# Banded attention heads in a fused transformer layer: where the division, the sinks, the low key halves and a norm are computed

## The chip, the cores and the metric

The kernel runs on one core of a Trainium2 chip. The core has five engines that run side by side and wait for each other by semaphores: TensorE (PE, matrix products into PSUM), VectorE (DVE), ScalarE (ACT), GpSimd (POOL) and SyncE (SP, which here only issues transfers). The metric is the device time of one launch in microseconds (us), lower is better.

## The reference, cut to what matters

One layer: modulated norm, one input projection, two groups of attention heads, output projection, residual, second modulated norm, and a mixture of 32 experts of which each token uses four. There are 512 tokens and 256 context tokens, width 1024. The change concerns the second group of heads, eight query heads over two key heads, banded, with a sink logit per head:

```python
s_loc = einsum('bnqkgd,bnjkd->bnkgqj', qbk, kband)      # own block of 128 tokens and its neighbours
s_ctx = einsum('bnqkgd,bjkd->bnkgqj', qbk, k_ctx)       # all 256 context tokens
s_loc = where(valid, s_loc, MASK_VALUE)
p = softmax(concatenate([s_loc, s_ctx, sink_col], -1), -1)   # the sink only enters the sum
o = einsum(p_loc, vband) + einsum(p_ctx, v_ctx)
...
x = x + g1 * (concatenate([ya, yb], -1) @ w_out)
hx2 = modulate(rmsnorm(x, norm2_g), sh2, sc2)           # then router logits, top 4 of 32
```

## The kernel before, in words

All products are in fp32 accuracy from parts: a value is split into a high part (a rounding copy, ScalarE) and a low part (the difference, VectorE), and the products of the parts are added in PSUM. Weights go through the same split.

The launch has three stretches. First the modulation, the input projection and the four global heads. Then the stage of the banded heads, in which the output projection, the second norm and the router of the blocks already finished run along. Last the experts: for each, 24 weight tiles of 1024 columns are split by ScalarE and VectorE and multiplied by TensorE, while the SP queue loads the next ones into buffers as they come free.

The banded stage walks through sixteen units (n, m): n is a block of 128 tokens, m a pair of the eight query heads. A unit of block 0 or 3 has 512 keys, one of block 1 or 2 has 640. `scores_B` makes a unit's scores: for each of two heads and each cut of the keys (256 and 256, or 256, 256 and 128 for the first head and 256 and 384 for the second with 640 keys) a product with the high keys on 128 rows (`kB[:, g]`, to which the queries hold both their halves) and one with the low keys on the 64 rows on which they lie (`kB[rw, 2]`), then masks in bf16. A one-column copy of the sink goes beside the scores, then maximum, exponential with its sum, reciprocal, and the scaling of the probabilities, on VectorE for one head and on ScalarE for the other. The tiles `sc` (scores) and `o` (values) exist once in PSUM, `tp` (transposes) and `pj` (projections) twice. `turn_B` transposes the probabilities two key blocks at a time and splits them, `mix_B` multiplies them with the values, `put_B` adds the two halves of a finished pair of units into `yB` and splits the result for the output projection. `start_Y` splits the global heads' rows for the same product.

A loop over the units makes the next unit's scores while it turns and mixes the current one, and puts the output projection's parts (`out_proj`, one of eight row blocks kb), and the steps `norm2`, `route_T`, `route` and `rank` of the block before, in between. The scheduler reorders each engine's instructions by a model of the machine, with the written order as priority; only what is marked with `keep_in_program_order` or pinned stays put. The two last row blocks of block 3's projection, and all that prepares the first expert, stand behind the loop and are pinned. The new helper names in the diff replace these functions.

Of the kernel before, what the change touches and what calls it, by code (L numbers as in the profile page):

```python
# [10 lines left out]
F32 = mybir.dt.float32  # L11
F32R = mybir.dt.float32r
# [10 lines left out]
T = 512  # L23
# [14 lines left out]
def tile_block(ctx: ExitStack, tc: tile.TileContext, a: dict, out: bass.AP, dbg=None):  # L38
# [64 lines left out]
    def ps_pj():  # L103
        return ps.tile([128, 512], F32, name="pj", bufs=2)
# [704 lines left out]
    def scores_B(n, m):  # L809

        b0, b1 = max(n - 1, 0), min(n + 2, 4)
        L = (b1 - b0) * 128
        nk = C + L
        g = m // 2
        rw = slice(g * 64, g * 64 + 64)
        q = qT[n]
        own = n + m < KN["own"]
        if own:
            assert nk == 512
            sv = [ps_pj() for _ in range(2)]  # L820
        else:
            s = sc_tile(KN["sB"])
            sv = [s[:, 0:TA], s[:, TA:2 * TA]]
        for i in range(2):
            hd, s = 2 * m + i, sv[i]
            cuts = [(0, C), (C, nk)] if i == 1 or nk == 512 else [(0, C), (C, 512), (512, nk)]
            masks = []
            if n > 0:
                masks.append((mprev, C))
            if n < 3:  # L830
                masks.append((mnext, nk - 128))
            ksl = lambda x0, x1: slice(T + x0, T + x1) if x0 < C else slice(b0 * 128 + x0 - C, b0 * 128 + x1 - C)
# [8 lines left out]
        nm = bp.tile([128, 2], F32, name="nmB", bufs=4)  # L841
        rs = bp.tile([128, 2], F32, name="rsB", bufs=4)
        w = nk if own else nk + 1
        for i in range(0 if own or KN["snk"] == "P" else 2):
            (V.tensor_copy if KN["snk"][i] == "V" else S.copy)(sv[i][:, nk:w], sinkB[:, 2 * m + i:2 * m + i + 1])
        for i in range(2):
            V.tensor_reduce(nm[:, i:i + 1], sv[i][:, 0:w], axis=AX.X, op=OP.max, negate=True)
        if own:
            es = bp.tile([128, 3, 2], F32, name="esB", bufs=1)
            V.tensor_scalar_mul(es[:, 0], sinkB[:, 2 * m:2 * m + 2], -1.0)  # L850
            V.tensor_tensor(nm, nm, es[:, 0], op=OP.min)
            V.tensor_add(es[:, 1], nm, sinkB[:, 2 * m:2 * m + 2])
            S.activation(es[:, 2], es[:, 1], AF.Exp)
        pp = []
        for i in range(2):
            p = bp.tile([128, 641], F32, name="pB", bufs=5)
            S.activation(p[:, 0:w], sv[i][:, 0:w], AF.Exp, bias=nm[:, i:i + 1], accum_out=rs[:, i:i + 1])
            pp.append(p)
        if own:
            V.tensor_add(rs, rs, es[:, 2])  # L860
        V.reciprocal(rs, rs)
        for i in range(2):
            if KN["scB"][i] == "S":
                S.activation(pp[i][:, 0:nk], pp[i][:, 0:nk], AF.Copy, scale=rs[:, i:i + 1])
            else:
                (V if KN["scB"][i] == "V" else G).tensor_scalar(pp[i][:, 0:nk], pp[i][:, 0:nk], rs[:, i:i + 1], 1.0,
                                                             op0=OP.mult, op1=OP.mult)
        return pp, [4, 5] + list(range(b0, b1))

    def turn_B(pp, bl):  # L870

        w = len(bl) * 256
        tp = ps_tp().rearrange("p a b -> p (a b)")
        for i, x in enumerate(bl):
            for j in range(2):
                PE.transpose(tp[:, (2 * i + j) * 128:(2 * i + j + 1) * 128], pp[j][:, x * 128:(x + 1) * 128], ident)
        pt = pair(bp, [128, 512], "pT", 2)
        split(pt[0][:, 0:w], pt[1][:, 0:w], tp[:, 0:w])
        return pt
# [49 lines left out]
    cur = scores_B(0, 0)  # L929
# [72 lines left out]
    Gt = lp.tile([128, E], F32, name="Gt")  # L1002
# [10 lines left out]
    fill = lp.tile([128, E * 3], F32, name="fill")  # L1013
    V.memset(fill, 0.0)
# [19 lines left out]
    zt = lp.tile([128, D], F32, name="t1", bufs=2)  # L1034
    V.memset(zt, 0.0)
    dma(acc[T:T + 128, :], zt)
# [20 lines left out]
    def norm2(t):  # L1057
        t1 = lp.tile([128, D], F32, name="t1", bufs=2)
        for f in range(2):
            add_out(t, f, t1)  # L1060
        late = V if t == 3 else G
        gp2(t1, x1[t], G2B, OP.mult)
        sq = lp.tile([128, 4, 128], F32, name="ya", bufs=1).bitcast(BF16).rearrange("p a b -> p (a b)")
        ss = lp.tile([128, 1], F32, name="ss2", bufs=2)
        rs = lp.tile([128, 1], F32, name="rs2", bufs=2)
        S.activation(sq, x1[t], AF.Square, accum_out=ss)
        rstd_of(rs, ss, D)

        rt[t] = t1, rs, late
# [53 lines left out]
    def enter_slots(t):  # L1123
        eq, mi, ge, gs, pr = rt.pop(t)
        pk = lp.tile([128, 4, E], F32, name="pk")
# [13 lines left out]
        V.tensor_mul(eq, eq, val[:, :, 1:2].to_broadcast([128, 4, E]))  # L1139
        V.tensor_reduce(Gt, eq.rearrange("p k e -> p e k"), axis=AX.X, op=OP.add)  # L1140
# [29 lines left out]

    for i, (n, m) in enumerate(units):
        nxt = scores_B(*units[i + 1]) if i < 15 else None
        if m % 2 == 0:
            o = ps_o()
        pp, blocks = cur
        if m == 0 and n > 0:
            start_Y(n)
        if n == 0 and m == KN["ys"][0]:
            start_Y(n, slice(0, KN["yh"]))
        if n == 0 and m == KN["ys"][1]:  # L1180
            start_Y(n, slice(KN["yh"], 4))
# [12 lines left out]
        if m % 2 == 1:  # L1194
            put_B(m // 2, o, Yt[n][1])
# [3 lines left out]
        if n == 0 and m == 2:  # L1199
            router_vectors()  # L1200
# [4 lines left out]
        if n > 0:  # L1205
            (norm2, route_T, route, rank)[m](n - 1)
# [4 lines left out]
        if m == 3 and n < 2:  # L1211
            load_qB(n + 2)
    most = mo.tile([1, 1], I32, name="most")
# [644 lines left out]
```

## Time and profile before

| | us |
|---|---|
| median of three timed runs | 1682.74 |
| lowest and highest of them | 1678.67, 1683.17 |
| the profiled execution | 1678.89 |
| its span, first to last instruction | 1677.1 |
| banded stage in it | 285 to 457 |

Times inside the profile count from the first instruction. An engine's busy time is the sum of its instructions' durations, which for TensorE overlap, so the start of the next one is the better measure there. PEld is TensorE's loading of the stationary operand. Most instructions carry line 52, a helper through which they are all recorded, and are told apart by the tiles that they write and read (out<-in).

### The profile page before, as it was taken

How to read it: one execution, taken by the hardware profiler on the slowest of the kernel's cores; microseconds unless marked ns; L12 is line 12 of the kernel's file. 1: busy time of each engine (PE TensorE's matmuls, PEld its weight loads, DVE VectorE, ACT ScalarE, POOL GpSimd, SP SyncE). 2: the span in 40 equal slices, each digit the busy share in tenths (PEclk: the TensorE clock that was granted, in tenths of full speed). 3: DMA queues.
4: the chain of work that ended last, by engine and by line, in shares of the span. 5: the costliest groups of instructions: out<-in, count | busy, mean ns of one | idle time of the engine just before them, and what ended most of it. 6: DMA issues, size and time to landing. Idle time of an engine off the chain costs nothing. (4 is left out here: it accounts for less than half of the span.)

```text
span 1677.1 us, 20947 instructions
## 1 busy us (share of the span) xinstructions
PE 1601.9 (96%) x7464; PEld 1283.1 (77%) x7464; DVE 1482.5 (88%) x1753; ACT 1093.5 (65%) x1406; POOL 213.6 (13%) x136
## 2 busy tenths in 40 slices
PE   7899997899889999999999999999999999999995
PEld 2686775677677888888888888888888888888884
DVE  6888887556778999999999999999999999999995
ACT  6544434445556767777776777776777777677763
POOL 0000001012330111111111111111111111111011
PEclk9899997879979999999999999999999999999998
DMA  9534325611579999999999999999999999999974
GB/s 350 173 92 132 108 88 149 184 45 47 193 244 380 353 367 369 357 377 372 374 362 366 360 369 380 383 362 366 369 362 369 374 374 361 367 355 370 357 295 128
DMA packets 115698, 494.11 MB, mean 295 GB/s; under 512 B 16385, under 2 KB 39082, under 8 KB 68418
## 3 DMA queue, kind: packets, MB, share of 16 engines
q1 hardware_dynamic: 99090, 456.44, 71.2%
q0 software_dynamic: 14192, 29.00, 8.4%
q10 hardware_dynamic: 2304, 7.24, 1.2%
q8 instruction: 61, 1.00, 0.2%
q14 instruction: 51, 0.42, 0.1%
HBM read 472.91 MB, written 27.57 MB: 298 GB/s over the span
## 5 line engine op out<-in xcount | busy, mean ns | idle before, releaser
L52 PE MATMUL h<-two 128*128 128x512 f32 x1694 | 421.5, 400 | 3.0 <-ACT two L52 3.0
L52 PEld LDWEIGHTS h<-two 128*128 128x128 f32 x1694 | 315.3, 189 | 74.3 <-ACT two L52 3.9
L52 PE MATMUL h<-wp,two 128*128 128x512 f32 x1338 | 334.7, 400 | 4.1 <-DVE pk L52 4.1
L52 DVE TENSOR_TENSOR two<-wp,two 128x1024 fp32r<-128x1024 f32 x254 | 300.8, 1219 | 7.5 <-ACT two L52 7.4
L52 PEld LDWEIGHTS h<-wp,two 128*128 128x128 f32 x1338 | 249.1, 190 | 58.2 <-ACT two L52 4.3
L52 ACT CAST two<-wp 128x1024 fp32r<-128x1024 f32 x254 | 258.0, 1049 | 17.0 <-PE y L52 14.6
L52 DVE TENSOR_TENSOR wp<-wp 128x1024 fp32r<-128x1024 f32 x176 | 205.5, 1219 | 2.9 <-ACT wp L52 2.9
L52 DVE TENSOR_TENSOR two<-w,two 128x1024 fp32r<-128x1024 f32 x170 | 200.2, 1219 | 2.3 <-ACT two L52 2.3
L52 POOL DMA_INDIRECT acc<-ys,slot_i x31 | 105.5, 3403 | 704.6 <-DVE ys L52 704.6
L52 ACT CAST wp<-wp 128x1024 fp32r<-128x1024 f32 x176 | 176.2, 1050 | 12.2 <-PE y L52 7.1
L52 ACT CAST two<-w 128x1024 fp32r<-128x1024 f32 x170 | 170.2, 1049 | 13.3 <-PE y L52 10.5
L52 PE MATMUL y<-two,ah 128*128 128x512 f32 x556 | 174.6, 395 | 0.8 <-DVE w L52 0.8
L52 PE MATMUL y<-wp,ah 128*128 128x512 f32 x468 | 147.1, 395 | 0.4 <-DVE wp L52 0.4
L52 DVE TENSOR_TENSOR wp<-w,wp 128x1024 fp32r<-128x1024 f32 x104 | 125.5, 1218 | 8.4 <-ACT wp L52 8.3
L52 PEld LDWEIGHTS y<-two,ah 128*128 128x128 f32 x556 | 104.4, 188 | 26.1 <-DVE w L52 1.2
L52 ACT CAST wp<-w 128x1024 fp32r<-128x1024 f32 x104 | 108.7, 1049 | 23.4 <-PE pj L52 10.3
L52 ACT CAST ah<-tpm 128x512 fp32r<-128x512 f32 x64 | 37.6, 588 | 123.1 <-PE tpm L52 123.1
L52 PE MATMUL y<-two,al 128*128 128x512 f32 x278 | 109.9, 395 | 0.0
L52 PEld LDWEIGHTS y<-wp,ah 128*128 128x128 f32 x468 | 88.2, 188 | 21.3 <-DVE wp L52 0.6
L52 DVE TENSOR_TENSOR wp<-wchunk,wp 128x1024 fp32r<-128x1024 f32 x82 | 98.2, 1218 | 0.0
L52 PE MATMUL pj<-xh,wp 128*128 128x512 f32 (+1 forms) x320 | 91.7, 364 | 1.9 <-ACT xf L52 1.0
L52 PE MATMUL y<-wp,al 128*128 128x512 f32 x234 | 92.4, 395 | 0.0
(333 smaller groups left out, 2350.1 us busy)
## 6 DMA issues: line engine op xcount, KB each, us to landing
wp<-in_w_gate_up_dram SPq DMA_DIRECT2D x140, 1024.0 KB
w<-in_w_gate_up_dram SPq DMA_DIRECT2D x85, 1024.0 KB
wp<-in_w_down_dram SPq DMA_DIRECT2D x75, 1024.0 KB
w<-in_w_down_dram SPq DMA_DIRECT2D x43, 1024.0 KB
wchunk<-in_w_gate_up_dram SPq DMA_DIRECT2D x31, 1024.0 KB
wm<-in_w_mod_dram SPq DMA_DIRECT2D x64, 256.0 KB
wchunk<-in_w_down_dram SPq DMA_DIRECT2D x10, 1024.0 KB
w<-in_w_in_dram SPq DMA_DIRECT2D x14, 512.0 KB
```

Source lines behind the costliest of these rows:

```text
L52: i = f(*args, **kwargs)
```

## The change

- The low keys get a tile of their own, `klB`, padded with zeros to 128 rows for each key head, and the second score product reads all 128 rows.
- The sink column is written by a small matmul (three bf16 parts of the sink on rows 0, 32 and 64, against ones), in all units but the first.
- The probabilities are not scaled any more. `put_B` takes the reciprocals of four heads' sums, broadcasts them by four transposes into a `tp` tile, and multiplies the finished values.
- The second norm's factor (`norm2_factor`) is computed one unit later than its square sum.
- Small tiles of the router share buffers, a zero tile is smaller and is read twice.
- `Scores` and `Turned` replace `scores_B` and `turn_B` by steps that the loop calls one by one; the loop puts them, and the steps of projection, norm and router, in another order.

```diff
+    klB = bp.tile([128, 2, TA], F32R, name="klB")
+    for g in range(2):
+        rw, ro = slice(g * 64, g * 64 + 64), slice(64 - g * 64, 128 - g * 64)
+        G.memset(klB[ro, g].bitcast(F32), 0.0)
+        S.copy(klB[rw, g], kB[rw, 2].bitcast(F32))
...
             for x0, x1 in cuts:
                 PE.matmul(s[:, x0:x1], q[:, hd], kB[:, g, ksl(x0, x1)], start=True, stop=False)
-                PE.matmul(s[:, x0:x1], q[rw, hd], kB[rw, 2, ksl(x0, x1)], start=False, stop=not mk)
+                PE.matmul(s[:, x0:x1], q[:, hd], klB[:, g, ksl(x0, x1)], start=False, stop=not mk)
-            if not own and KN["snk"] == "P":
+            if not self.own:
                 PE.matmul(s[:, nk:nk + 1], ones3, sink3[:, hd:hd + 1], start=True, stop=True)
-        for i in range(0 if own or KN["snk"] == "P" else 2):
-            (V.tensor_copy if KN["snk"][i] == "V" else S.copy)(sv[i][:, nk:w], sinkB[:, 2 * m + i:2 * m + i + 1])
...
-        V.reciprocal(rs, rs)
-        for i in range(2):
-            if KN["scB"][i] == "S":
-                S.activation(pp[i][:, 0:nk], pp[i][:, 0:nk], AF.Copy, scale=rs[:, i:i + 1])
-            else:
-                (V if KN["scB"][i] == "V" else G).tensor_scalar(pp[i][:, 0:nk], pp[i][:, 0:nk], rs[:, i:i + 1], 1.0,
-                                                             op0=OP.mult, op1=OP.mult)
...
+        def exp(self, i):
+
+            p = bp.tile([128, 641], F32, name="pB", bufs=4)
+            S.activation(p[:, 0:self.w], self.sv[i][:, 0:self.w], AF.Exp, bias=self.nm[:, i:i + 1], accum_out=self.rs[:, i:i + 1])
+            self.pp.append(p)
...
+    class Turned:
+
+
+        def __init__(self, pp, bl):
+            self.w = len(bl) * 256
+            self.tp = ps_tp().rearrange("p a b -> p (a b)")[:, 0:self.w]
+            for i, x in enumerate(bl):
+                for j in range(2):
+                    PE.transpose(self.tp[:, (2 * i + j) * 128:(2 * i + j + 1) * 128], pp[j][:, x * 128:(x + 1) * 128], ident)
+
+        def high(self):
+            self.pt = pair(bp, [128, 512], "pT", 2)
+            S.copy(self.pt[0][:, 0:self.w], self.tp)
+
+        def low(self):
+            V.tensor_tensor(self.pt[1][:, 0:self.w], self.tp, self.pt[0][:, 0:self.w].bitcast(F32), op=OP.subtract)
...
-    def put_B(g, o, y):
+    def put_B(n, g, o, y):
...
+        rs = sums[n, g]
+        V.reciprocal(rs, rs)
+        rb = ps_tp()
+        for j in range(4):
+            PE.transpose(rb[:, j, :], rs[:, j:j + 1].to_broadcast([128, 128]), ident)
         S.copy(yb[0:64], ov[64:128, 0::2, :])
         S.copy(yb[64:128], ov[0:64, 1::2, :])
         V.tensor_add(yb[0:64], ov[0:64, 0::2, :], yb[0:64])
         V.tensor_add(yb[64:128], ov[64:128, 1::2, :], yb[64:128])
+        V.tensor_mul(yb[0:64], yb[0:64], rb[0:64, 0::2])
+        V.tensor_mul(yb[64:128], yb[64:128], rb[64:128, 1::2])
         fb = slice(4 + 2 * g, 6 + 2 * g)
         split(y[:, 0, fb], y[:, 1, fb], yb)
...
-    cur = scores_B(0, 0)
+    cur = Scores(0, 0)
...
-    fill = lp.tile([128, E * 3], F32, name="fill")
-    V.memset(fill, 0.0)
+    zt = lp.tile([128, 4, 128], F32, name="hT", bufs=1).rearrange("p a b -> p (a b)")
+    V.memset(zt, 0.0)
+    fill = zt[:, 0:E * 3]
...
-    zt = lp.tile([128, D], F32, name="t1", bufs=2)
-    V.memset(zt, 0.0)
-    dma(acc[T:T + 128, :], zt)
+    dma(acc[T:T + 128, :].rearrange("p (a f) -> p a f", a=2), zt[:, None, :].to_broadcast([128, 2, 512]))
...
+        S.activation(sq, x1[t], AF.Square, accum_out=ss)
+        rt[t] = t1, ss, late
+
+    def norm2_factor(t):
+        t1, ss, late = rt[t]
         rs = lp.tile([128, 1], F32, name="rs2", bufs=2)
-        S.activation(sq, x1[t], AF.Square, accum_out=ss)
         rstd_of(rs, ss, D)
...
-        lg = lp.tile([128, E], F32, name="lg", bufs=2)
+        lg = lp.tile([128, E], F32, name="lg", bufs=1)
...
-        pk = lp.tile([128, 4, E], F32, name="pk")
+        pk = lp.tile([128, 4, 128], F32, name="hT", bufs=1)[:, 0].rearrange("p (k e) -> p k e", k=4)
...
+        Gt = lp.tile([128, E], F32, name="lg", bufs=1)
...
-        nxt = scores_B(*units[i + 1]) if i < 15 else None
+        nxt = Scores(*units[i + 1]) if i < 15 else None
...
-        pp, blocks = cur
-        if m == 0 and n > 0:
-            start_Y(n)
-        if n == 0 and m == KN["ys"][0]:
-            start_Y(n, slice(0, KN["yh"]))
-        if n == 0 and m == KN["ys"][1]:
-            start_Y(n, slice(KN["yh"], 4))
+        pp, blocks = cur.pp, cur.blocks
         fill = [(n - 1, 6), (n - 1, 7)] if m == 0 else [(n, 2 * m - 2), (n, 2 * m - 1)]
-        if n == 0:
-            fill = [(0, kb) for kb in KN["f0"][m]]
+        if n + m == 0:
+            fill = []
         bls = [list(range(x, min(x + 2, len(blocks)))) for x in range(0, len(blocks), 2)]
-        pts = [turn_B(pp, bl) for bl in bls[:2]]
-        for k, bl in enumerate(bls):
-            if k == 2:
-                pts.append(turn_B(pp, bl))
-            if k < len(fill):
-                out_proj(fill[k][0], [fill[k][1]])
-            mix_B(m, pts[k], bl, blocks, o)
-        cur = nxt
-        if m % 2 == 1:
-            put_B(m // 2, o, Yt[n][1])
+        if nxt:
+            for k in range(2):
+                nxt.head(k)
+            for k in range(2):
+                nxt.max(k)
+        ts = [Turned(pp, bl) for bl in bls[:2]]
+        for k in range(2):
+            ts[k].high()
+            if nxt:
+                nxt.exp(k)
+        for k in range(2):
+            ts[k].low()
+        if m != 1:
+            for f in fill[0:1]:
+                out_proj(f[0], [f[1]])
+        mix_B(m, ts[0].pt, bls[0], blocks, o)
+        if len(bls) > 2:
+            ts.append(Turned(pp, bls[2]))
+            ts[2].high()
+            ts[2].low()
+
+        if m == 0:
+            start_Y(n, slice(0, 4 if n else 3))
+        if (n, m) == (0, 2):
+            start_Y(n, slice(3, 4))
         if n == 0 and m < 3:
             prep_out(2 * m + 2)
             prep_out(2 * m + 3)
-        if n == 0 and m == 2:
+        if (n, m) == (0, 3):
             router_vectors()
         if n > 1 and m == 0:
             turn_gates(n - 2)
             start_acc(n - 2, ps_tp)
             load_x1(n)
-        if n > 0:
-            (norm2, route_T, route, rank)[m](n - 1)
+        if n > 0 and m == 1:
+            norm2(n - 1)
+        if n > 0 and m == 2:
+            norm2_factor(n - 1)
+            route_T(n - 1)
+        if n > 0 and m == 3:
+            route(n - 1)
+        if m != 1:
+            for f in fill[1:2]:
+                out_proj(f[0], [f[1]])
+        for k in range(1, len(bls)):
+            mix_B(m, ts[k].pt, bls[k], blocks, o)
+        if m == 1:
+            for f in fill:
+                out_proj(f[0], [f[1]])
+        if m % 2 == 1:
+            put_B(n, m // 2, o, Yt[n][1])
+        if n > 0 and m == 3:
+            rank(n - 1)
+        cur = nxt
         if m == 2 and n < 3:
             load_Y(n + 1)
             if n == 0:
                 load_x1(1)
         if m == 3 and n < 2:
             load_qB(n + 2)
+    pinned[0] = ""
```

## Rows read from the trace of the kernel before

**Rows 1.** The page, busy time of each engine over the whole span (share of the span, instructions).

```profile
PE 1601.9 (96%) x7464; PEld 1283.1 (77%) x7464; DVE 1482.5 (88%) x1753; ACT 1093.5 (65%) x1406; POOL 213.6 (13%) x136
```

**Rows 2.** Busy time of each engine in stretches (from:to, length, busy us and instructions of each engine, granted TensorE clock as a share of 2.4 GHz, DMA share, GB/s): the banded stage, three slices of it, a slice of the experts.

```profile
285.00:457.00 172.00, 157.35 (x803) 121.93 (x802) 111.34 (x259) 87.92 (x200) 31.75 (x30) 0.90 0.37 115
285.00:295.00 10.00, 7.87 (x38) 5.64 (x37) 8.65 (x16) 4.90 (x10) 0.00 (x0) 0.84 0.45 145
335.00:345.00 10.00, 8.69 (x32) 5.99 (x31) 6.15 (x10) 5.88 (x12) 0.00 (x0) 0.58 0.19 60
415.00:425.00 10.00, 8.92 (x63) 7.21 (x61) 6.35 (x23) 5.10 (x15) 0.00 (x0) 1.00 0.09 26
1000.00:1010.00 10.00, 10.00 (x48) 8.27 (x47) 9.38 (x10) 7.54 (x10) 1.33 (x1) 1.00 1.02 390
```

**Rows 3.** Who waited for whom (us in total, times, longest): TensorE in the banded stage, its two longest entries, and the SP queue from 500 to 1640 us.

```profile
PE sc L52 <- ACT pB L52: 2.3, 5, 0.8
PE o L52 <- DVE pTl L52: 2.3, 5, 0.7
...
SPq L1257 <- DVE two L52: 316.5, 127, 5.3
```

**Rows 4.** Matmuls in order of time, at full clock (start, us from the first start to the last end of the merged ones, instruction, count). First a chain of value products (the first and the last of five that follow each other), then groups of score products and masks of two units.

```profile
365.52 0.27 PE L52 MATMUL o<-pTl,vB 128*128 128x256 f32 x1
...
365.99 0.28 PE L52 MATMUL o<-pTl,vB 128*128 128x256 f32 x1
...
319.02 1.32 PE L52 MATMUL sc<-kB,qB 128*128 128x256 f32 x4 [0.47 <-ACT pB L52]
320.27 0.23 PE L52 MATMUL sc<-mprev,identb 128*128 128x128 bf16 x1
320.31 0.56 PE L52 MATMUL sc<-kB,qB 128*128 128x128 f32 x2
320.80 0.23 PE L52 MATMUL sc<-mnext,identb 128*128 128x128 bf16 x1
...
368.76 1.42 PE L52 MATMUL sc<-kB,qB 128*128 128x256 f32 x4
370.10 0.23 PE L52 MATMUL sc<-mprev,identb 128*128 128x128 bf16 x1
```

**Rows 5.** Groups of instructions in the banded stage (count, busy us, mean ns of one, idle time before them and its causes).

```profile
L52 PE MATMUL sc<-kB,qB 128*128 128x256 f32 (+5 forms) x136 | 47.8, 406 | 2.3 <-ACT pB L52 2.3
L52 PE MATMUL o<-pTh,vB 128*128 128x256 f32 x72 | 23.4, 338 | 2.6 <-DVE yB L52 1.3 <-ACT pTh L52 1.1
L52 ACT ACTIVATE pB<-pB,rsB 128x512 f32<-128x512 f32 (+1 forms) x16 | 12.5, 780 | 4.6 <-DVE rsB L52 4.6
L52 DVE TENSOR_SCALAR pB<-pB,rsB 128x512 f32<-128x512 f32 (+1 forms) x16 | 9.5, 597 | 0.3
L52 DVE TENSOR_TENSOR yB<-o,yB 64x256 f32<-64x256 f32 x16 | 6.7, 422 | 7.9 <-ACT yB L52 7.5
L52 DVE COPY sc<-sinkB 128x1 f32<-128x1 f32 x15 | 2.4, 163 | 15.4 <-PE sc L52 15.3
L52 PE MATMUL tp<-bdr,GtT 96*128 96x512 f32 x4 | 1.4, 398 | 0.0
```

**Rows 6.** Score products in order of time in the half-clock stretch.

```profile
338.87 2.30 PE L52 MATMUL sc<-kB,qB 128*128 128x256 f32 x4
341.11 0.29 PE L52 MATMUL sc<-mprev,identb 128*128 128x128 bf16 x1
```

**Rows 7.** Score products of a global head in order of time: two on 128 rows, two on 64, and the next.

```profile
262.54 0.61 PE L52 MATMUL sc<-kh,q 128*128 128x512 f32 x2 [2.11 <-ACT p L52]
263.08 0.61 PE L52 MATMUL sc<-kl,q 64*128 64x512 f32 x2
263.62 0.61 PE L52 MATMUL sc<-kh,q 128*128 128x256 f32 x2
```

**Rows 8.** Broadcast transposes of a global head's factors and what follows them, in order of time.

```profile
308.13 0.65 PE L52 MATMUL tp<-ident,rr 128*128 128x128 f32 x4 [1.45 <-POOL rr L52]
308.62 0.60 PE L52 MATMUL tp<-ident,pB 128*128 128x128 f32 x4
```

**Rows 9.** The first unit's score products, and a memset on GpSimd behind the stage, in order of time.

```profile
272.39 1.09 PE L52 MATMUL pj<-kB,qB 128*128 128x256 f32 x2 [1.52 <-DMA qB<-qB_d]
...
460.69 1.80 POOL L52 MEMSET bg<- 64x2048 f32 x1
```

**Rows 10.** One unit's reciprocal and scaling, and the sink copies and the maximum of the next, in order of time.

```profile
396.36 0.16 DVE L52 RECIPROCAL rsB<-rsB 128x2 f32<-128x2 f32 x1
...
397.02 0.55 DVE L52 TENSOR_SCALAR pB<-pB,rsB 128x640 f32<-128x640 f32 x1
...
402.81 0.16 DVE L52 COPY sc<-sinkB 128x1 f32<-128x1 f32 x1 [0.51 <-PE sc L52]
...
403.48 1.54 DVE L52 TENSOR_REDUCE nmB<-sc 128x1 f32<-128x641 f32 x2
```

**Rows 11.** The end of the stage in order of time: the split of the last value tile and the projection's last products.

```profile
456.11 0.43 DVE L52 TENSOR_TENSOR two<-yB,two 128x256 fp32r<-128x256 f32 x1
...
456.30 1.20 PE L52 MATMUL pj<-w,two 128*128 128x512 f32 x2
```

More of the change, by code (lines that the diff above doesn't have):

```diff
@@ L807, in tile_block @@
     V.tensor_sub(sink3[64:65], sinkr, sink3[32:33])
[L809 to L820, printed above, removed]
-        else:
-            s = sc_tile(KN["sB"])
-            sv = [s[:, 0:TA], s[:, TA:2 * TA]]
-        for i in range(2):
-            hd, s = 2 * m + i, sv[i]
-            cuts = [(0, C), (C, nk)] if i == 1 or nk == 512 else [(0, C), (C, 512), (512, nk)]
-            masks = []
-            if n > 0:
[L829 to L832, printed above, removed]
+    klB = bp.tile([128, 2, TA], F32R, name="klB")
@@ new lines, in tile_block, with __init__, head @@
+    for g in range(2):
+        rw, ro = slice(g * 64, g * 64 + 64), slice(64 - g * 64, 128 - g * 64)
+        G.memset(klB[ro, g].bitcast(F32), 0.0)
+        S.copy(klB[rw, g], kB[rw, 2].bitcast(F32))
+    class Scores:
+        def __init__(self, n, m):
+            self.n, self.m = n, m
+            self.b0, b1 = max(n - 1, 0), min(n + 2, 4)
+            self.blocks = [4, 5] + list(range(self.b0, b1))
+            self.nk = len(self.blocks) * 128
+            self.own = n + m == 0
+            if self.own:
+                self.sv = [ps_pj() for _ in range(2)]
+            else:
+                s = sc_tile(KN["sB"])
+                self.sv = [s[:, 0:TA], s[:, TA:2 * TA]]
+            self.w = self.nk if self.own else self.nk + 1
+            self.nm = bp.tile([128, 2], F32, name="nmB", bufs=4)
+            if m % 2 == 0:
+                sums[n, m // 2] = bp.tile([128, 4], F32, name="rsB", bufs=3)
+            self.rs = sums[n, m // 2][:, m % 2 * 2:m % 2 * 2 + 2]
+            self.pp = []
+        def head(self, i):
+            n, m, nk, s = self.n, self.m, self.nk, self.sv[i]
+            hd, g, q = 2 * m + i, m // 2, qT[n]
+            cuts = [(0, C), (C, nk)] if i == 1 or nk == 512 else [(0, C), (C, 512), (512, nk)]
+            masks = ([(mprev, C)] if n > 0 else []) + ([(mnext, nk - 128)] if n < 3 else [])
+            ksl = lambda x0, x1: slice(T + x0, T + x1) if x0 < C else slice(self.b0 * 128 + x0 - C, self.b0 * 128 + x1 - C)
@@ L835, in scores_B @@
                 mk = [(mt_, y) for mt_, y in masks if x0 <= y < x1]
-                PE.matmul(s[:, x0:x1], q[rw, hd], kB[rw, 2, ksl(x0, x1)], start=False, stop=not mk)
+                PE.matmul(s[:, x0:x1], q[:, hd], klB[:, g, ksl(x0, x1)], start=False, stop=not mk)
                 for j, (mt_, y) in enumerate(mk):
                     PE.matmul(s[:, y:y + 128], identb, mt_, start=False, stop=j == len(mk) - 1)
-            if not own and KN["snk"] == "P":
+            if not self.own:
                 PE.matmul(s[:, nk:nk + 1], ones3, sink3[:, hd:hd + 1], start=True, stop=True)
-        nm = bp.tile([128, 2], F32, name="nmB", bufs=4)
@@ L842, in scores_B @@
-        rs = bp.tile([128, 2], F32, name="rsB", bufs=4)
-        w = nk if own else nk + 1
-        for i in range(0 if own or KN["snk"] == "P" else 2):
-            (V.tensor_copy if KN["snk"][i] == "V" else S.copy)(sv[i][:, nk:w], sinkB[:, 2 * m + i:2 * m + i + 1])
[L846 to L860, printed above, removed]
-        V.reciprocal(rs, rs)
-        for i in range(2):
-            if KN["scB"][i] == "S":
-                S.activation(pp[i][:, 0:nk], pp[i][:, 0:nk], AF.Copy, scale=rs[:, i:i + 1])
-            else:
-                (V if KN["scB"][i] == "V" else G).tensor_scalar(pp[i][:, 0:nk], pp[i][:, 0:nk], rs[:, i:i + 1], 1.0,
-                                                             op0=OP.mult, op1=OP.mult)
@@ L868, in scores_B, with max @@
[L868 to L879, printed above, removed]
+        def max(self, i):
+            V.tensor_reduce(self.nm[:, i:i + 1], self.sv[i][:, 0:self.w], axis=AX.X, op=OP.max, negate=True)
@@ new lines, in sinks @@
+        def sinks(self):
+            self.es = bp.tile([128, 3, 2], F32, name="esB", bufs=1)
+            V.tensor_scalar_mul(self.es[:, 0], sinkB[:, 2 * self.m:2 * self.m + 2], -1.0)
+            V.tensor_tensor(self.nm, self.nm, self.es[:, 0], op=OP.min)
+            V.tensor_add(self.es[:, 1], self.nm, sinkB[:, 2 * self.m:2 * self.m + 2])
+            S.activation(self.es[:, 2], self.es[:, 1], AF.Exp)
+        def exp(self, i):
+            p = bp.tile([128, 641], F32, name="pB", bufs=4)
+            S.activation(p[:, 0:self.w], self.sv[i][:, 0:self.w], AF.Exp, bias=self.nm[:, i:i + 1], accum_out=self.rs[:, i:i + 1])
+            self.pp.append(p)
@@ new lines, in tile_block @@
+    sums = {}
+    class Turned:
[10 more added lines that the diff above has]
+            V.tensor_tensor(self.pt[1][:, 0:self.w], self.tp, self.pt[0][:, 0:self.w].bitcast(F32), op=OP.subtract)
@@ L928, in tile_block @@
         pass
-    cur = scores_B(0, 0)
+    cur = Scores(0, 0)
+    for i in range(2):
+        cur.head(i)
+    for i in range(2):
+        cur.max(i)
+    cur.sinks()
+    for i in range(2):
+        cur.exp(i)
+    V.tensor_add(cur.rs, cur.rs, cur.es[:, 2])
     for f in later:
@@ L1001, in tile_block @@
     V.memset(zrow, 0.0)
-    Gt = lp.tile([128, E], F32, name="Gt")
     g3 = lp.tile([128, 3, E], F32R, name="g3")
@@ L1204, in tile_block @@
             load_x1(n)
-        if n > 0:
-            (norm2, route_T, route, rank)[m](n - 1)
+        if n > 0 and m == 1:
[18 more added lines that the diff above has]
+        cur = nxt
         if m == 2 and n < 3:
```

## The prediction, on record before the change was run

> **What bounds the kernel now.** I read the page first. TensorE is busy for 96% of the span, VectorE for 88% [rows 1]. Those are averages over two very different parts. The second part, from about 500 us on, is the experts: a slice from its middle shows TensorE busy for all of its ten microseconds at full clock and VectorE for 9.4, and the queue that loads the weights waits there for VectorE to free split tiles, not for memory [rows 2, 3]. That part has no slack and the diff doesn't touch it; whatever comes out ahead of it moves its start, and the weights' loads start earlier too, since they wait for buffers. So the question is the stage of the banded heads, 285 to 457 us, in which all sixteen units run.
>
> In that stage TensorE is busy for 157 of 172 us, VectorE for 111 and ScalarE for 88 [rows 2]. A matmul's recorded duration overlaps the next one's, so I read starts. Five value matmuls of 256 columns start 0.12 us apart [rows 4]. Four score matmuls of the same 256 columns, which alternate between 128 and 64 rows, take 1.25 us from the first start to the mask behind them, 0.31 us each [rows 4]. Nobody is waited for there; the same work goes through at under half the rate. A group with two of 256 columns and two of 384 takes 1.34 us, a pair of 128 columns 0.49 us [rows 4]. The list of waits has no cause above 2.3 us in total for TensorE in the stage [rows 3]. TensorE is therefore the bound over most of the stage. The exception is its beginning, where the last global head still runs: there the engine is 79% busy [rows 2], and gaining its time buys little.
>
> **The change part by part.** Terms are in TensorE time, since that engine sets the stage's end.
>
> *Low keys on 128 rows.* The second matmul of each pair reads 64 rows of queries and keys; now it reads 128, the other half of the keys being zero. By the code eight units have 640 keys and ten score matmuls (six of 256 columns, two of 384, two of 128) and seven in the stage have 512 keys and eight of 256: 104, 16 and 16, together the 136 of the trace [rows 5]. At full clock each 256-column one should fall from 0.31 to 0.12, 0.19 less; 384 columns from (1.34 - 2 x 0.31) / 2 = 0.36 to 0.12 x 1.5 = 0.18; 128 columns from 0.245 to the 0.12 of a transpose of that width [rows 8], 0.12. Sum: 104 x 0.19 + 16 x 0.18 + 16 x 0.12 = 24.6 us. The lower end leaves out the sixteen of the stage's beginning (3 us): 21.6. The upper end adds the half-clock stretches, where four of them take 2.24 us, 0.56 each [rows 6]; with a mean granted clock of 0.90 [rows 2] that is a fifth of the stage: 29. I take 23. The first unit's eight lie ahead of the stage, behind a wait for their queries [rows 9], and count nothing.
>
> What speaks against this edit is the Trainium skill, "TensorEngine Tiling (Array Packing)", section Theoretical Speedup: a contraction of at most 64 rows can run up to twice as fast, which padding to 128 throws away. By that rule the edit would cost up to 68 x 0.06 = 4 us instead of saving 23. The rows show no such gain: in the global heads two 64-row matmuls of 512 columns take 0.54 us, and the two 128-row ones before them also 0.54 [rows 7].
>
> *The zero-padded keys.* Two GpSimd memsets of 64x768 (1.80 us for 2048 columns [rows 9], so 0.7 each) and two ScalarE copies (under 1.0 each, by the scalings of up to 640 columns [rows 5]). They can run while the first banded scores wait 1.5 us for the queries' transfer [rows 9]: nothing; without that cover 1.7 us once.
>
> *Sinks by TensorE.* Thirty one-column matmuls on 96 rows, a size that the trace of before lacks. Lower bound: behind a bf16 mask the next matmul starts 0.04 us later [rows 4], 30 x 0.04 = 1.2. Upper bound: if 96 rows cost what 64 do, once going in and once coming out, 30 x 2 x 0.19 = 11. The one 96-row form that the trace has lasts 398 ns for 512 columns, while the score matmuls last 406 for mostly 256 and the value matmuls 338 [rows 5]; that is nearer to the undisturbed ones, and I take +1.2. In exchange 15 copies each go from VectorE (2.4 us [rows 5]) and ScalarE, and with them 0.67 us of a unit's chain, from the first copy to the maximum [rows 10].
>
> *Division behind the values.* Gone are 16 scalings on ScalarE (12.5 us), 16 on VectorE (9.5 us) [rows 5] and eight of 16 reciprocals of 0.16 us, all between the exponentials and the transposes: 1.2 us from the reciprocal to the end of the scaling [rows 10]. New are eight times four broadcast transposes on TensorE, four in 0.49 us [rows 8]: 32 x 0.12 = +3.9; and 16 VectorE products of 64x256, which I price as the additions of that shape, 0.42 each, 6.7 us [rows 5]. VectorE falls from 111 to about 105, ScalarE from 88 to about 73; neither becomes the bound of a stage of some 150 us. The products lie on the path only at the very end: the last projection products wait for the split of the last value tile [rows 11], so two more products there are +0.8. The other seven pairs are hidden behind the next unit's scores and projections.
>
> *Second norm in two steps.* VectorE's step on the square sum and GpSimd's power move one unit later, so that VectorE's queue doesn't stand behind ScalarE's square sum. VectorE has 60 us free in the stage [rows 2]: nothing. The shared scratch tiles of the router and the smaller zero tile wait for tiles long read; at most a few tenths.
>
> *Order and chain.* The hand-written sequence (scores and maxima of the next unit, transposes, high halves between exponentials) sets the scheduler's priorities. A unit's chain is 0.67 + 1.2 = 1.9 us shorter. TensorE's waits on that chain (for exponentials and low halves) add up to 4.6 us [rows 3], and what the half clock costs comes on top, about 8. Between 0 and 12.6; I take 3.5, since a faster TensorE also meets new waits.
>
> Sum: -23 + 1.2 + 3.9 + 0.8 - 3.5 = -20.6 us. The profiled execution took 1678.9 us, 1.8 of it outside its span; it agrees with the lowest of the three timed runs, and the middle of all four is 1680.8. From that: **1660 us**.
>
> **The rivals.** *A larger gain* (chance 0.17): low keys at their upper 29, all 4.6 us of waits, and 6 us of the half clock back: 29 - 5.9 + 4.6 + 6 = 34 less, 1647. For it: a chain 1.9 us shorter in every unit. Against: waits seldom go altogether.
>
> *The freed time becomes a wait* (0.16). The broadcast reciprocals hold one of two transpose banks until both products are done, at least 0.85 us of additions and 0.85 of products. If the next unit's transposes wait behind that in the seven inner places, 7 x 1.7 = 12 us return: 9 less, 1672. Against: scores and projections stand ready for TensorE in that time.
>
> *Slower* (0.09), by the clock alone: a TensorE with less to do per unit pauses more, and more of the stage is granted 1.2 instead of 2.4 GHz, as in the slice from 335 us at 0.58 after a busy share of 8.7 of 10 [rows 2]. The score group then needs 2.24 instead of 1.25 us, so each microsecond there loses up to half. The stage has some 34 us of it now; it ends slower once more than 41 further us fall there, and with 60 at 1690. Against: the slice from 415, with 8.9 of 10 busy, is granted 1.00 [rows 2].
> The Trainium skill, "TensorE: Matmul & The Clock Gate", Part 4, says that a transpose does not count as busy for the gate in the same way; the 32 added ones would push towards this case. No run here shows that.
>
> **How the numbers follow.** Forecast (gain 13 to 30) 0.58, larger 0.17, a new wait 0.16, slower 0.09. The range from 1640 (41 less) to 1674 (7 less) holds the first two and more than half of the third. Faster by over 0.3% (5 us, about what a measurement of this kernel can tell from no change): 0.58 + 0.17 + 0.11 = 0.86; within 0.3%: 0.05 of the new wait and 0.03 of the slow case, 0.08; slower 0.06.
>
> **What would show it.** In the profile after, four 256-column score matmuls within about 0.5 us; no scaling of the probabilities; 32 more broadcast transposes at 0.12; the stage some 20 us shorter and the experts' part as long as before, only earlier. Wrong would be: score matmuls still 0.2 us or more apart, 96-row matmuls with the gap of the 64-row ones, transposes waiting for a bank that the reciprocals hold, or more half clock than now.

## The result, and the profile after

The changed kernel took 1671.92 us in the median of five runs (1667.94 to 1673.79), the kernel before 1682.33 beside it (1678.62 to 1683.17): a ratio of 0.9942 with the interval [0.9922, 0.9963]. It is faster, as forecast, but by 10 us where 21 were forecast. The profiled execution took 1673.35 us, its span is 1671.6; against the one before (1678.89) that is 5.5 us, since the profiled one is among the slower of the runs of the changed kernel and among the faster of the other. One run of all that follow (1963.76 us at a mean granted clock of 0.743, with the sinks copied) was slow, and is left out of medians and ratios.

The page's busy line, which answers to [rows 1]:

```profile
PE 1580.4 (95%) x7526; PEld 1278.3 (76%) x7526; DVE 1477.6 (88%) x1729; ACT 1083.3 (65%) x1377; POOL 215.5 (13%) x138
```

TensorE is busy 21.5 us less over the span, although it runs 62 instructions more, and the span is only 5.5 us shorter. The stretches, which answer to [rows 2] (the first from the first score in `sc` to the split of the last value tile; columns as there):

```profile
281.80:448.20 166.40, 138.24 (x860) 118.69 (x859) 104.57 (x227) 76.32 (x169) 29.90 (x28) 0.92 0.38 119
335.00:345.00 10.00, 10.00 (x63) 8.72 (x62) 6.43 (x13) 4.64 (x10) 3.29 (x2) 1.00 0.08 28
...
500.00:1600.00 1100.00, 1097.95 (x4948) 897.99 (x4947) 1047.05 (x970) 804.81 (x877) 139.16 (x59) 1.00 0.98 368
```

TensorE is busy for 138 of 166 us, 83%, where it was 157 of 172, 91%: it has less to do and stands idle more. The granted clock of the stage is about the same on average (0.92 and 0.90). The first expert product starts at 480.3 us instead of 485.8, and from it to the end of the span both kernels take 1191.3 us.

TensorE in order of time around the end of a pair of units, at full clock, which answers to [rows 4, 8] (start, length, instruction, count):

```profile
409.12 0.28 PE L52 MATMUL o<-pTl,vB 128*128 128x256 f32 x1
409.24 0.60 PE L52 MATMUL tp<-ident,rsB 128*128 128x128 f32 x4
409.59 0.36 PE L52 MATMUL sc<-kB,qB 128*128 128x256 f32 x1
409.79 0.28 PE L52 MATMUL sc<-klB,qB 128*128 128x256 f32 x1
409.91 0.28 PE L52 MATMUL sc<-kB,qB 128*128 128x256 f32 x1
410.03 0.28 PE L52 MATMUL sc<-klB,qB 128*128 128x256 f32 x1
410.15 0.23 PE L52 MATMUL sc<-mprev,identb 128*128 128x128 bf16 x1
410.22 0.17 PE L52 MATMUL sc<-sink,ones 96*128 96x1 bf16 x1
410.25 0.36 PE L52 MATMUL sc<-kB,qB 128*128 128x256 f32 x1
...
413.02 1.50 PE L52 MATMUL tp<-ident,pB 128*128 128x128 f32 x8 [1.92 <-DVE yB L52]
```

Four score products of 256 columns take 0.56 us to the mask, not 1.25 to 1.34. Four broadcast transposes take 0.35 us, and a sink product 0.03 to the next start. These TensorE prices are about those of the forecast. Then the engine runs dry: the next transposes wait for VectorE's work on `yB`. VectorE in the same stretch:

```profile
410.21 0.87 DVE L52 TENSOR_TENSOR yB<-o,yB 64x256 f32<-64x256 f32 x2
411.12 0.16 DVE L52 RECIPROCAL gs<-gs 128x1 f32<-128x1 f32 x1
411.31 0.41 DVE L52 TENSOR_TENSOR yB<-yB,tp 64x256 f32<-64x256 f32 x1
411.65 0.68 DVE L52 TENSOR_REDUCE nmB<-sc 128x1 f32<-128x513 f32 x1
412.25 0.17 DVE L52 TENSOR_TENSOR pos<-tp,selb 128x32 f32<-128x32 f32 x1
412.45 0.42 DVE L52 TENSOR_TENSOR yB<-yB,tp 64x256 f32<-64x256 f32 x1
412.91 0.29 DVE L52 TENSOR_TENSOR hT<-eq,tp 128x128 f32<-128x128 f32 x1
...
413.25 0.68 DVE L52 TENSOR_REDUCE nmB<-sc 128x1 f32<-128x513 f32 x1
```

The factors' transposes end at 409.84 us. Between the two products VectorE puts a maximum and a router step, so their bank is free at 412.87 only, 3.0 us later. The next unit's second maximum has moved behind the second product.

TensorE's waits from 281 to 449 us, which answer to [rows 3] (the three longest):

```profile
PE o L52 <- DVE pTl L52: 5.7, 6, 1.5
PE o L52 <- DVE yB L52: 3.3, 3, 1.7
PE tp L52 <- DVE yB L52: 3.2, 2, 1.9
```

They stood at 2.3 for `pTl`, 1.3 for `o` behind `yB` [rows 5], and no entry for `tp` behind `yB`.

**Where TensorE's time went.** I added up the times from each matmul's start to the next, from 270 us to the first expert product. What a matmul of that width takes in a chain at full clock is work; what follows a change between 64 and 128 rows is switch; what a 1.2 GHz stretch adds to the work is half clock; the rest is idle. The split hangs on what is taken as a matmul's price in a chain; it is an estimate, good to some three or four microseconds (the switches to one). The sums begin with the first matmul behind 270 us. The kernels in the middle are those of the experiments below ("+ division" is the low keys with the division alone).

| us | before | low keys alone | + division | changed, no products | changed | changed, 64-row keys |
|---|---|---|---|---|---|---|
| work | 132.4 | 133.2 | 135.5 | 136.5 | 137.0 | 137.3 |
| switch | 28.1 | 0.4 | 0.4 | 0.4 | 0.4 | 28.2 |
| half clock | 22.0 | 15.4 | 14.5 | 13.9 | 20.2 | 28.1 |
| idle | 33.2 | 43.5 | 47.2 | 43.9 | 51.6 | 37.6 |
| sum | 215.7 | 192.5 | 197.8 | 194.9 | 209.2 | 231.2 |

Work rose by 4.6 us, against 5.1 forecast for sinks and transposes. The switches gave 27.7. Idle time took 18 back. By the split of the value tiles, the changed kernel was 18.5 us ahead after four of the eight pairs (372.0 against 390.5), and 7.9 after all of them (448.2 against 456.1). The granted clock is a part of this:

```profile
285.00:390.50 105.50, 96.04 (x463) 73.57 (x462) 65.78 (x141) 52.67 (x116) 13.05 (x16) 0.84 0.36 103
390.50:457.00 66.50, 61.31 (x342) 48.35 (x341) 45.56 (x119) 35.25 (x84) 18.71 (x15) 0.99 0.37 132
```

```profile
281.80:372.00 90.20, 74.61 (x484) 65.32 (x484) 56.41 (x111) 43.91 (x95) 9.47 (x12) 0.91 0.41 121
372.00:449.00 77.00, 63.62 (x379) 53.37 (x376) 48.96 (x119) 32.40 (x74) 20.82 (x17) 0.92 0.35 119
```

These are the kernel before and then the changed one, split at the fourth pair (columns as in [rows 2]). In its first half the change meets a higher clock than the kernel before (0.91 for 0.84), in its second a lower one (0.92 for 0.99).

### The profile page after: what moved, and what is told of

Read it like the earlier page. It is cut to its first block, busy times and chain, and to the rows that moved or that the text cites. A ratio compares the mean times of both kernels' runs of the same rounds, so it can differ in the third digit from the quotient of the medians.

```text
span 1671.6 us, 21059 instructions
## 1 busy us (share of the span) xinstructions
PE 1580.4 (95%) x7526; PEld 1278.3 (76%) x7526; DVE 1477.6 (88%) x1729; ACT 1083.3 (65%) x1377; POOL 215.5 (13%) x138
## 5 line engine op out<-in xcount | busy, mean ns | idle before, releaser
L52 ACT CAST ah<-tpm 128x512 fp32r<-128x512 f32 x64 | 37.6, 588 | 123.0 <-PE tpm L52 123.0
```

What stands on the lines that cost most here:

```text
L52: i = f(*args, **kwargs)
```

## The experiments

Three series, each beside its own runs of the kernel before (medians 1680.11, 1679.7 and 1679.26). Differences between kernels are taken from the ratios, times 1680 us.

### One part after the other, in the old order

The first kernel has only the smaller and shared tiles (four buffers for the probabilities, shared router tiles, the smaller zero tile), so that the rest fits. The second adds the low keys:

```diff
-                PE.matmul(s[:, x0:x1], q[rw, hd], kB[rw, 2, ksl(x0, x1)], start=False, stop=not mk)
+                PE.matmul(s[:, x0:x1], q[:, hd], klB[:, g, ksl(x0, x1)], start=False, stop=not mk)
```

The third adds the sinks by TensorE (`'snk': 'VS'` becomes `'snk': 'P'`), the fourth the division behind the values (the scalings go, `put_B` is that of the changed kernel).

> The kernel before with only the shared small tiles, the smaller zero tile and four instead of five probability tiles, as the room for the padded keys needs them. Theory one (TensorE time falls as counted, and the written order gives the gain back): within 3 us of before, ratio 0.998 to 1.002. Theory two (the stage hangs on the chain through VectorE and ScalarE anyway): one probability tile less can make it up to 5 us slower.

> The run with the shared tiles, and the low keys padded to 128 rows; loop order, sinks and scaling as before. Theory one: 16 to 23 us less than before (ratio 0.986 to 0.990), more than the whole change, since TensorE is the bound in this order. Theory two: 3 to 8 us less, the rest turns into TensorE's waits at once.

> The same and the sinks written by TensorE; 30 matmuls more, 30 one-column copies less; scaling and loop order as before. Theory one: 2 us less to 1 us more than the run before it. Theory two: 5 us or more less, since the chain of every unit is 0.67 us shorter.

> The same and the division behind the values; only the loop order and the norm's second step are still those of before. Theory one: 2 to 6 us more than the run before it (32 transposes, and the bank that they hold), so about 1665, below the whole change by 5 us or more. Theory two: less than the run before it by 5 us or more, since the chain of every unit is 1.2 us shorter.

| kernel | median us | ratio to before | 95% |
|---|---|---|---|
| tiles | 1678.79 | 0.9999 | 0.9979 to 1.0018 |
| + low keys on 128 rows | 1651.3 | 0.9834 | 0.9807 to 0.9862 |
| + sinks by TensorE | 1657.53 | 0.9881 | 0.9852 to 0.9910 |
| + division behind the values | 1666.24 | 0.9930 | 0.9903 to 0.9956 |
| the changed kernel | 1671.92 | 0.9942 | 0.9922 to 0.9963 |

The low keys alone bring 28 us, more than the whole change and more than the 16 to 23 expected. Every later part takes some of it back, by the medians; from the low keys on, the intervals of neighbouring rows overlap, but the one with the division is clear of the low keys alone. Neither theory had the sinks (at most 1 us slower, or 5 faster): they cost 7.9. The division costs 8.2, where the first theory had 2 to 6. The kernel with the low keys alone beats both kernels.

Part of these differences goes with the clock. The median of the runs' mean granted clock is 0.970 before, 0.979 with the low keys alone and 0.973 in the changed kernel. Single runs at 0.975 or 0.976 took 1674.86 us before, 1655.73 with the low keys alone and 1670.08 in the changed kernel: 19 us gained and 14 lost again, where the ratios have 28 and 18. The kernels keep their order; how much of the rest a lower clock brings, and how much idle time brings the lower clock, no run separates.

### One part undone or alone, around the changed kernel

The changed kernel with the old second score product (the line above, reversed):

> The changed kernel with one line back: the low keys' score product reads 64 rows again (the padded tile is made but not read). Theory one (low keys are the whole gain, everything else of the change costs): TensorE gets back about 28 us of row switches, the idle time that the change brought takes at most a few us of it, so about 1692 us, slower than before (1680 to 1682). Theory two (the rest of the change has a chain of waits that would set the stage's end anyway, so that the switches hide in its idle time): within 8 us of the changed kernel's 1672.

It took 1696.85 us, ratio 1.0102 [1.0079, 1.0126]: slower than before. Its score products in order of time, four of 256 columns again 1.23 us from the first start to the mask:

```profile
410.79 1.30 PE L52 MATMUL sc<-kB,qB 128*128 128x256 f32 x4
412.02 0.23 PE L52 MATMUL sc<-mprev,identb 128*128 128x128 bf16 x1
412.08 0.17 PE L52 MATMUL sc<-sink,ones 96*128 96x1 bf16 x1
```

So the low keys are worth 27 us (0.0160 of 1680) in the new order too, as theory one had it (the profiled executions are 21 us apart). The last column of the table above shows how: 28 of switches and 8 of half clock come back, and 14 us of idle time go, where the theory had a few.

The changed kernel with no division at all (reciprocals, broadcast transposes and products left out):

```diff
-        V.reciprocal(rs, rs)
-        rb = ps_tp()
-        for j in range(4):
-            PE.transpose(rb[:, j, :], rs[:, j:j + 1].to_broadcast([128, 128]), ident)
...
-        V.tensor_mul(yb[0:64], yb[0:64], rb[0:64, 0::2])
-        V.tensor_mul(yb[64:128], yb[64:128], rb[64:128, 1::2])
```

> The changed kernel without any division: no reciprocals, no broadcast transposes, no products, so the banded heads' values stay unnormalised. Theory one (the division behind the values costs its TensorE work of 4 us and about 5 us of waits on the bank and the products): about 1663 us, and no entry of transposes waiting for yB. Theory two (the new order is what costs): 1667 us or more, since only the transposes' 4 us go.

1658.41 us, ratio 0.9858 [0.9833, 0.9883]: 14 us less than the changed kernel, more than theory one asked. The values stay unnormalised, but the experts' part takes as long as before (1191.2 us in the profile), so the times can be compared. In the new order the division is the larger part of what was lost.

The changed kernel with sinks and division as before, so that low keys, loop order and split norm stay (the removed lines of the diff, as a step `scale` behind the two exponentials):

> The changed kernel with sinks by copies and the division ahead of the transposes, as before: what stays is the low keys on 128 rows, the new loop order and the norm in two steps. If the new order costs by itself: some 6 us above the kernel with the low keys alone (1651), about 1657 to 1660. If it is neutral and only division and sinks cost: 1651 within 3. If it only works with the division behind the values, whose shorter chain it was written for: 1665 or more.

1657.64 us, ratio 0.9871 [0.9847, 0.9894]: 6 us above the low keys alone, as if the new order cost something by itself, but the intervals overlap.

The low keys with the division alone, in the old order (the fourth kernel of the first series with `'snk': 'VS'`):

> The kernel before with the low keys on 128 rows and the division behind the values, sinks still by copies, the order of the loop as before. If the division costs 9 us by itself, as between the kernels with and without it that have sinks by TensorE: 1660 us. If it costs only its 4 us of transposes: 1655. If the sinks by TensorE are needed for it to be bad: 1652 or less.

1662.05 us, ratio 0.9897 [0.9875, 0.9918]: the division costs 10.6 us by itself, and the interval lies clear of the low keys' own.

### Inside the division, and the size of small things

The changed kernel with reciprocals and transposes, without the products (the last two lines of the diff above):

> The changed kernel with the reciprocals and their broadcast transposes, but without the 16 products on VectorE: the values stay unnormalised. Without all three it took 1658.4 us, with all three 1672. Theory one (the products are what costs: the next unit's low halves queue behind them on VectorE, and they hold the transposes' bank): 1660 to 1664, the 4 us of transposes above the kernel without any. Theory two (the transposes cost it, by their place in TensorE's queue or by what they wait for): 1668 or more.

1657.5 us, ratio 0.9875 [0.9847, 0.9904], clear of the changed kernel's 0.9942 [0.9922, 0.9963], and lower than theory one had it. The 32 transposes and the reciprocals cost 3 us by the ratios (nothing is within the intervals), the 16 products 11. Runs at the same clock say it too: 1657.41 and 1659.31 us at 0.976, the changed kernel 1670.08 at 0.975. The products' own VectorE time is 6.7 us:

```profile
L52 DVE TENSOR_TENSOR yB<-yB,tp 64x256 f32<-64x256 f32 x16 | 6.7, 416 | 0.4
```

This row is the changed kernel's, by tile and shape (count, busy us, mean ns). TensorE's waits in the kernel without the products, from 281 to 449 us:

```profile
PE tp L52 <- DVE g L52: 5.3, 1, 5.3
PE o L52 <- DVE pTl L52: 2.8, 5, 1.5
...
PE o L52 <- DVE yB L52: 1.8, 3, 1.3
```

The first entry lies behind this kernel's stage (at 439.8 us); the changed kernel has 4.6 us of it behind 449. The entry of transposes behind `yB` is gone (3.2 us), low halves fall from 5.7 to 2.8, `o` behind `yB` from 3.3 to 1.8: 7.6 us, which is about the idle time that the products bring in the table (51.6 against 43.9). Of the 14 us between the two sums of the table another 6 are half clock.

The changed kernel with the sinks copied as before:

```diff
-            if not self.own:
-                PE.matmul(s[:, nk:nk + 1], ones3, sink3[:, hd:hd + 1], start=True, stop=True)
...
+            if not self.own:
+                hd = 2 * self.m + i
+                (V.tensor_copy if i == 0 else S.copy)(self.sv[i][:, self.nk:self.w], sinkB[:, hd:hd + 1])
```

> The changed kernel with the sinks copied by VectorE and ScalarE as before. If the sinks by TensorE cost some 5 us here too, as they did ahead of the division and in the old order (6 and 4): 1667. If that cost was the scheduler's order for those kernels alone: 1672 within 3, or above, since TensorE's products are replaced by copies that lengthen the chain of a unit by 0.67 us.

1662.84 us, ratio 0.9904 [0.9875, 0.9934], less than either case expected. The sinks by TensorE cost 6.4 us here, 7.9 behind the low keys and 5.5 behind the division: three times the same sign, though no pair of intervals is clear of the other. At the same clock (0.975 or 0.976) they cost 1 to 4 us behind the low keys (1657.04 and 1659.72 against 1655.73) and 7 here (1670.08 against 1662.74).

The low keys with the norm in two steps (`norm2_factor` ahead of `route_T`, one unit behind `norm2`):

> The kernel before with the low keys on 128 rows and the second norm in two steps, nothing else. If this edit is free, as forecast: 1651 within 3. It is also the smallest edit of all: if it moves the time by 5 us or more, a good part of the other edits' prices is what any edit does to the scheduler's order.

1653.49 us, ratio 0.9846 [0.9818, 0.9874]: free within the intervals, as forecast. This smallest edit moved the time by 2 us; what the scheduler makes of a larger one is not bounded by that.

The low keys with both scalings on ScalarE (`'scB': 'VS'` becomes `'SS'`):

> The kernel before with the low keys on 128 rows, and both scalings of the probabilities on ScalarE instead of one on each. VectorE then has some 10 us less in the stage, ScalarE 12 more. If the new idle time of TensorE is a wait on VectorE's queue (low halves behind the scaling): faster than 1651, to 1645. If the chain of a unit sets it (both scalings one after the other on one engine, 0.78 us later): slower, 1655 to 1662.

1661.95 us, ratio 0.9895 [0.9868, 0.9921]: 10 us slower. VectorE had 10 us less to do, and TensorE waited about as long for its low halves as before and longer for ScalarE's high halves. First the low keys alone, then this kernel, TensorE's waits from 281 to 449 us, the two longest of each:

```profile
PE o L52 <- DVE pTl L52: 6.4, 10, 2.2
PE o L52 <- DVE yB L52: 3.7, 5, 1.6
```

```profile
PE o L52 <- DVE pTl L52: 5.4, 10, 1.1
PE o L52 <- ACT pTh L52: 5.1, 8, 1.7
```

So it isn't VectorE's load that sets the stage once the score products are fast: the changed kernel has 113 us of it in the 180 from 285 us, and the one with the new order alone, which is 12 us faster by the ratios, has 134. What fits these runs is the order of steps of one unit: maximum, exponential, scaling, transposes, high half, low half, values. The products, put among these steps, cost 11 us for 6.7 us of busy time; the scaling, which went to the engine that does the exponentials and high halves, cost 10. No run changes this chain alone, so it stays an explanation.

## Why the prediction was right and wrong

**Right: the bound, the sign, and the low keys.** TensorE was the bound of the stage before, and its score products went at less than half their rate for nothing but the change of rows. I took 23 us; the chip gave 27.7 (tiles to low keys) and 26.9 (changed kernel against its 64-row form). The mechanism was right and the size a little low: the upper bound of 29 (its own rows give about 28: a fifth of the sum, with 0.32 us saved for each product instead of 0.19) was the nearer one. The rule of the Trainium skill that I set against it ("TensorEngine Tiling (Array Packing)", section Theoretical Speedup: up to twice as fast with at most 64 rows) would, by the prediction's estimate, have made the padding cost up to 4 us. It saved 27, and the measurement decides: narrow products between wide ones lost more here than they could win.

The reading of [rows 7] against that rule was wrong, though, since a merged line carries its first shape alone. The same stretch of the kernel before by shape, 262.4 to 264.6 us:

```profile
L52 PE MATMUL sc<-kh,q 128*128 128x512 f32 x2 | 0.9, 444 | 2.1 <-ACT p L52 2.1
L52 PE MATMUL sc<-kl,q 64*128 64x512 f32 x2 | 0.9, 442 | 0.0
...
L52 PE MATMUL sc<-kh,q 128*128 128x256 f32 x2 | 0.7, 333 | 0.0
L52 PE MATMUL sc<-kl,q 64*128 64x256 f32 x2 | 0.7, 328 | 0.0
```

Each pair is one product of 512 columns and one of 256, not two of 512. On 128 rows only, such products start 0.23 and 0.12 us apart (medians of the stage's trace), so a pair would take 0.35; it takes 0.54. These heads pay 0.19 us too, once for each change of rows.

**Right: the prices on TensorE.** Sink products, broadcast transposes and padded keys cost the engine what the sum said (work +4.6 us). The keys' memsets and copies, four instructions, lay ahead of the first scores:

```profile
L52 ACT CAST klB<-kB x2: 828/830/832, 263.6 to 264.5; 64x768 fp32r<-64x768 f32 x2
L52 POOL MEMSET klB<- x2: 732/732/732, 263.8 to 264.6; 64x768 f32 x2
```

These rows of the changed kernel go by tile (least, median and most ns, first and last start).

**Wrong: "The other seven pairs are hidden behind the next unit's scores and projections."** This is the step that failed most. I priced two products at 0.8 us at the very end and hid the rest by the time that TensorE would have work. But what they delay isn't TensorE's present work; it is VectorE's queue, in which the next unit's maxima and low halves stand, and the bank that the next transposes need. Measured: 11 us for the products, and for the whole division 8 to 11 in the old order and 14 in the new one, where the sum had 4.7. The fault was to go by VectorE's total (105 us in a stage of some 150): it had time to spare over the stage, and the products still came ahead of what TensorE waited for. That the products cost this is shown by leaving them out; that it goes through the queue is read from the rows and the waits (7.6 us), and a part of the rest stands as half clock.

**Wrong: "Order and chain", 3.5 us to the good.** I let the sum of TensorE's waits (4.6 us) shrink because a unit's chain becomes shorter by 1.9 us. The waits became longer: already the low keys alone, with the chain as it was, add 10 us of idle time. The likely reason is that TensorE, which needs 28 us less for the scores, arrives earlier at everything that it must wait for. The new order with the split norm added 6 us ahead of division and sinks, 1 behind the division (with copies), 2 behind both; whether it costs anything by itself is not settled, but no pair of kernels shows a gain.

**Wrong: the sinks.** Priced at +1.2 us less 0.67 of each unit's chain; measured 5.5 to 7.9 to the bad in three pairs. Their 30 products take TensorE only about 0.03 us each, as the chain row above shows. Why the kernel is slower all the same stays open: the profiled execution of the low keys with the sinks was the fastest of its five runs and has no more idle time than the low keys alone, and at the same clock only 1 to 4 us are left of its price.

**The rivals.** "The freed time becomes a wait" (0.16, 1672 us) gave the time that came. Its mechanism was half of it: the bank is held for 3.0 us in the rows above instead of the 1.7 that I took, but TensorE was seen waiting for it in two places only, 3.2 us in all. The other 4.4 of the 7.6 us that went with the products were waits for low halves and for `o` behind `yB`. The slower case by the clock didn't come: 20.2 us of half clock against 22.0. Part of it exists, though: of the 14 us between the table's sums with products and without, 6 are half clock. Whether the idle time brings it is not shown. The Trainium skill, "TensorE: Matmul & The Clock Gate", Part 4, says that transposes don't count as busy for the gate in the same way. The changed kernel without any division and the one with the 32 transposes, in that order, show no push from them (from 285 to 465 us, columns as in [rows 2]; the clock is 0.89 and then 0.91):

```profile
285.00:465.00 180.00, 152.49 (x922) 129.77 (x921) 117.78 (x242) 85.63 (x189) 39.97 (x40) 0.89 0.43 139
```

```profile
285.00:465.00 180.00, 151.62 (x954) 130.24 (x955) 117.99 (x254) 87.09 (x188) 39.66 (x40) 0.91 0.44 142
```

By parts, measured: -27.7 (low keys) + 7.9 (sinks) + 8.2 (division) + 2.0 (order and norm) = -9.6 us; forecast -23 + 1.2 + 4.7 - 3.5 = -20.6. That the range held the time is luck as far as the forecast's mechanism goes: it reached to 1674 for the sake of the rival.

**What the forecast said would show it.** Four score products in about half a microsecond, transposes at 0.12 or less, the experts' part unchanged: all there. "The stage some 20 us shorter" was true of its first half and was lost in the second. Transposes waiting for the bank that the reciprocals hold was named as what would make it wrong, and is there.

## What to carry to other kernels

Price a product that is moved off one path by the queue it is moved into: name what stands behind it on that engine and which bank it holds, and count until the last reader is done, with whatever the scheduler may put in between. When the bound engine gets much faster, the waits on the next chain can grow by themselves, as they did by 10 us here; a change that bundles one clear gain with several "free" moves should be run part by part, since here the first part alone, one score product on 128 rows, was worth 28 us and the bundle 10. Spare time of an engine over a stage says little about the chain through it: moving 10 us of scaling from VectorE to ScalarE made the kernel 10 us slower. Look at the granted clocks of the runs before a few microseconds are put down to an edit's own work.

## What was not expected of the hardware

Alternating 64-row and 128-row products cost TensorE 0.19 us each beside a chain on 128 rows only. A one-column product on 96 rows in bf16 between 128-row ones costs nothing of the kind: its neighbour starts 0.03 us later, and that neighbour's 0.20 us to its successor is what such a product takes behind a mask as well (390.18 to 390.38 us in the kernel with the low keys alone). The scatter of one kernel's runs follows the granted clock: of 17 runs of the kernel before, the one with the lowest mean clock (0.965) took 1685.53 us and the fastest (1671.13 us) had 0.974, close to the highest of 0.975.
